# Joined narrow score products, earlier state products and moved operand making in a block of two SwiGLUs around retention and pooling

## The chip, the cores and the metric

The kernel runs on one core of a Trainium2 chip. The metric is the time of one execution in device microseconds. TensorE (PE, with PEld for its weight loads), VectorE (DVE), ScalarE (ACT) and SyncE (SP, which here only issues DMAs) each work through a queue of their own in order, and meet at semaphores.

## The reference

One layer of a streaming encoder over 1024 tokens of width 1024, all in float32:

```python
h = x + 0.5 * swiglu(rmsnorm(x), ffn1_w_in, ffn1_w_out)        # inner width 2816
u = rmsnorm(h)
q, k, v, g_ret, p, gates = split(u @ w_in)                     # 4 heads of 256
ret = retention(rotary(q), rotary(k) / 16, v)                  # chunks of 64, decay per head
ret = ret * rsqrt(mean(ret * ret) + eps) * silu(g_ret)         # norm per head
pool = multiscale_pool(p, pool_w, pool_scale)                  # windows 2, 4, 8, 16
merged = sum_b(sigmoid(gate_b) * (branch_b @ w_up_b))          # branches ret and pool
h = h + merged @ w_out
h = h + 0.5 * swiglu(rmsnorm(h), ffn2_w_in, ffn2_w_out)
out = rmsnorm(h)
```

## The kernel before

**Products.** Every float32 operand is split into a rounded part "hi" and the rest "lo" (`split`: a cast on ScalarE, L161, and a subtraction on VectorE, L162; `split_scaled`, L165 and L166, multiplies by a scale as well). A product is three matmuls that add into one PSUM bank (`mm3`, L181 to L183): hi·hi, hi·lo, lo·hi. Each matmul has its own weight load. Nearly all large products go through Strassen's scheme, so sums and differences of quarters are made on VectorE before they are split: R11, R12, R21, R22 are the quarters of a normed activation, and T1 to T4 are the differences made from them (class `Next`, L268 on).

**Stages**, by the times of the profile: first half of SwiGLU 1 to about 470 us; its second half, tiles named b..., to 630; the values v to 715; the projections q, k, gates and pool rows to 1154; retention, with the pooling products as filler, to 1345; the merge, groups `ru` and `wo`, to 1520; SwiGLU 2, tiles c..., to 1890, and its second half, tiles d..., to the end.

**The order of the work.** The kernel is written as generators of steps (prep, body). `Flow.run` calls each step's prep four steps ahead of its body (LOOK = 4), and after each body takes one or two items from a background queue (`flow.add`, `Next.work`): the making of the next stage's operands, stores, statistics. The instruction order that results is then scheduled; what is made under `soon()` gets a high priority. Tiles come from rings of buffers (`tl` 4, `t4` 9, `c2` 8, PSUM 6 and 2), so a load or an instruction that takes a buffer waits for the last reader of what lay in it.

**Retention** (class `Unit`, L1446 on). A unit is one head h and one half nh of the tokens of each span, named 00, 01, 10, ... 31: eight units. `scores` makes, for j = 0 and 1, the decayed scores `sm` of a block of 128 keys against 256 and 128 queries: products into a bank `s`, then `sc`, scores times decay from PSUM (L1529), then the split into `sm`. j = 1 is the narrow one: 12 matmuls 128 wide. `keys` transposes k (L1434) and splits it with its decay into `kd`, in halves of 256 columns, ACT then DVE. `update` makes the state product `st` from `kd` and v, adds it to the running state `sf` (L1569) and splits that into `state`. `products` runs `update` and then the outputs `ob`: state times q (`across`) and scores times v (`inner`). `retention` (L1649 on) puts them in order: scores, keys, a filler (`fill`, 24 matmuls of the pooling products `pu`), then the rest. `finish` transposes the outputs (`ot`) and multiplies them by the gate `rg`, which is loaded for it.

**Values** (`values`, L1251 on). The product L11 is followed by the products S2 and S1 in turn; their weights are sums made on VectorE (L1271 to L1273) in the tiles `vL` and `vS`, split into `vS2w`, `vS1w`. Meanwhile the background queue makes R21 and T4 of the activation `n2` (`n2R21`, `n2T4`), queued at the end of SwiGLU 1 (`end_of`, L1114).

**Merge.** `handed` queues, between the pairs of groups, the operands of the next stage: for `wo` from `ru` (`mg`), for SwiGLU 2 from `wo` (`n3`). Of the first pair of groups nothing is made before the second pair begins.

**Last half of SwiGLU 2** (`ffn_out`, with `last`). Products P1, P6, P2, P7, P5, then P3 (tiles `dp3m`, `dp3w`, into the banks `dp5a` that P5 leaves), then P4 as steps `near(k)` and `far(n)` into the banks `n4s`. When P5's banks are evacuated, VectorE makes `dd` from them.

Of the kernel before, what the change touches and what calls it, by code (L numbers as in the profile page):

```python
# [17 lines left out]
P = 128  # L18
# [72 lines left out]
def block_kernel(ctx: ExitStack, tc, x, x_tok, vecs, f1_in, f1_out, w_in, w_v, pool_w, w_ret, w_pool, w_o,  # L91
# [180 lines left out]
    class Next(Norm):  # L272


        def __init__(self, name, gain, keep=None):
            super().__init__(name)
            self.gain, self.keep = gain, keep
            self.M, self.Y, self.made, self.ready, self.tiles, self.t1s, self.rb = {}, {}, {}, set(), {}, {}, None

# [39 lines left out]

        def t2(self, i):  # L320
            R11, R12, R22 = self.tiles[i, 0], self.tiles[i, 1], self.tiles[i + 4, 1]
            t1 = self.t1s[i] = c2(f"{self.name}t1{i}")
            tt(t1, R12, R11, SUB)

            self.less(R11, R22, t1, i)
            self.put("T2", i, R11)

        def t1(self, i):
            self.put("T1", i, self.t1s.pop(i), self.g(i))

        def t3(self, i):
            R12, R22 = self.tiles[i, 1], self.tiles[i + 4, 1]
            self.less(R12, R22, R12, i)
            self.put("T3", i, R12)
# [487 lines left out]
    def ffn_out(nx, ops, ready, w, res, name, sink, end, last=None):  # L822
# [196 lines left out]
        for k in range(FH):  # L1019
            yield step("p3", p3, k, "a", False, after3)  # L1020
        if not last:
            for k in range(1, FH):
                yield step("p4", p4, k, "b", False, after4)
            return
# [33 lines left out]

        for k in range(FH):
            yield near(k)  # L1060
# [53 lines left out]
    def end_of(nx):  # L1114
        def end(part):
            if part == 4:
                nx.work(nx.r21, nx.t4_)
            else:
                nx.work(*{2: (nx.r11,), 5: (nx.r22, nx.p22), 3: (nx.t2, nx.t1, nx.t3)}[part])

        return end

    end1 = end_of(mix)


# [116 lines left out]
    def values():  # L1242
# [97 lines left out]
        for p in zip(product("S2", "T2", "a", False, after6), product("S1", "T1", "b", True, after5)):  # L1340
            yield from p
# [104 lines left out]
    class Unit:  # L1446


        def __init__(self, h, nh):
            self.h, self.nh, self.name = h, nh, f"{h}{nh}"  # L1450
# [61 lines left out]
        def scores(self):  # L1512

            self.sm = []
            for j in range(2):
                wid = SPAN - j * P
                b = bank(f"s{self.name}{j}")
                for s in range(2):
                    at = s * SPAN + j * P
# [6 lines left out]
                with soon():  # L1526
                    for s in range(2):
                        at = slice(s * wid, (s + 1) * wid)
                        stt(c[:, at], b[:, at], self.row(8, 2 * s + j), self.dec[:, :wid], MUL, MUL)  # L1529
# [51 lines left out]

        def products(self):
            self.ob = {}
            mid = self.update(0)
            if self.nh == 1:
                self.across(0, self.state)
            else:
                self.state = self.update(1)
            for s in range(2):
                self.inner(s)  # L1590
            self.across(1, mid)
# [49 lines left out]
    def retention():  # L1641
# [9 lines left out]
        for n, u in enumerate(units):  # L1651
            after = units[n + 1] if n + 1 < len(units) else None

            def scores(u=u, n=n):
                if u.nh == 1:
                    u.follow(units[n - 1])
                u.scores()

            def rest(u=u, after=after):
# [27 lines left out]
    def after(nx):  # L1687

        def t2(i):
            nx.r22(i)  # L1690
# [61 lines left out]
    def handed(nx, last):  # L1752
# [3 lines left out]
        def between(pair, n):  # L1756
            if pair == 0:
                return
# [203 lines left out]
```

## Time and profile before

| | |
|---|---|
| time, median of 3 runs (lowest, highest) | 2149.32 us (2148.17, 2150.93) |
| the profiled execution: its own time | 2149.24 us |
| its span in the profile | 2147.2 us |
| granted TensorE clock | 1.000 |
| busy: PE, PEld, DVE, ACT | 2134.6, 1812.8, 1871.7, 1100.8 us |
| chain that ended last | PE 93%, DVE 4% |

The profiled execution took 2.0 us more than its span, and it lies 0.08 us from the median. In the rows of the profile a matmul's duration is modelled and overlaps its neighbours: what a matmul costs in a row of matmuls is the distance from one start to the next.

### The profile page before, as it was taken

The page shows a single profiled execution, that of the slowest core. Times are in us where ns is not written, and L with a number is a line of the kernel's source. Part 1 is how long each engine was busy: PE and PEld are TensorE (multiplying, and loading weights), DVE is VectorE, ACT ScalarE, POOL GpSimd, SP SyncE. Part 2 cuts the span into 40 slices and gives each one's busy share as a digit, 9 for nine tenths or more (in the row PEclk, how much of TensorE's full clock was granted, in tenths as well). Part 3 has the DMA queues.
Part 4 walks back from the last instruction along what each step waited for, and adds up shares of the span by engine and source line. Part 5 has one row for each costly group of instructions (what it writes and reads, how often), then busy time and mean ns, then how long its engine had stood idle before and what let it go on. Part 6 is the DMA issues. An engine that isn't in the chain of part 4 may idle for free.

```text
span 2147.2 us, 30158 instructions
## 1 busy us (share of the span) xinstructions
PE 2134.6 (99%) x10830; PEld 1812.8 (84%) x10830; DVE 1871.7 (87%) x3344; ACT 1100.8 (51%) x2074; POOL 0.2 (0%) x4
## 2 busy tenths in 40 slices
PE   9999999999999999999999999999999999999998
PEld 7888888888887888888888888888888888888887
DVE  8798888997986799999988788899988988899796
ACT  8544444554653544545457653446644544455454
POOL 0000000000000000000000000000000000000000
PEclk9999999999999999999999999999999999999999
DMA  7232323585542333232337566624123232357542
GB/s 257 75 133 74 138 84 134 196 274 177 180 139 89 108 121 114 107 120 108 123 124 231 172 229 235 230 94 161 65 97 124 85 127 84 132 198 274 196 131 100
DMA packets 116102, 313.61 MB, mean 146 GB/s; under 512 B 12784, under 2 KB 17008, under 8 KB 115952
## 3 DMA queue, kind: packets, MB, share of 16 engines
q1 hardware_dynamic: 115376, 310.63, 41.9%
q8 instruction: 85, 1.39, 0.3%
q10 hardware_dynamic: 576, 1.05, 0.1%
q14 instruction: 65, 0.53, 0.1%
HBM read 220.93 MB, written 90.70 MB: 145 GB/s over the span
## 4 chain that ended last, share of the span: by engine, by line
PE 93%; DVE 4%; DMA 1%; ACT 1%; issue 0%; SPq 0%; DVEq 0%; ACTq 0%
PE c_b L181 2%; PE c_b L182 2%; PE c_b L183 2%; PE a_b L181 2%; PE a_b L182 2%; PE a_b L183 2%; PE c_e L181 2%; PE c_e L182 2%; PE c_e L183 2%; PE a_e L182 2%; PE a_e L181 2%; PE a_e L183 2%; PE a_a L181 1%; PE a_a L182 1%; PE a_a L183 1%; PE c_a L182 1%
## 5 line engine op out<-in xcount | busy, mean ns | idle before, releaser
L182 PE MATMUL c_b<-n3T,c_wS 128*128 128x512 f32 x176 | 68.6, 390 | 0.0
L183 PE MATMUL c_b<-n3T,c_wS 128*128 128x512 f32 x176 | 68.5, 389 | 0.0
L181 PE MATMUL c_b<-n3T,c_wS 128*128 128x512 f32 x176 | 68.2, 390 | 0.0
L181 PE MATMUL a_b<-n1T,a_wS 128*128 128x512 f32 x168 | 65.4, 389 | 0.0
L182 PE MATMUL a_b<-n1T,a_wS 128*128 128x512 f32 x168 | 65.4, 389 | 0.0
L183 PE MATMUL a_b<-n1T,a_wS 128*128 128x512 f32 x168 | 65.3, 389 | 0.0
L181 PE MATMUL a_a<-n1R,a_wL 128*128 128x512 f32 x120 | 46.7, 389 | 0.0
L182 PE MATMUL a_a<-n1R,a_wL 128*128 128x512 f32 x120 | 46.7, 389 | 0.0
L183 PE MATMUL a_a<-n1R,a_wL 128*128 128x512 f32 x120 | 46.7, 389 | 0.0
L182 PE MATMUL c_a<-n3R,c_wL 128*128 128x512 f32 x112 | 43.7, 390 | 0.0
L181 PE MATMUL c_a<-n3R,c_wL 128*128 128x512 f32 x112 | 43.6, 389 | 0.0
L183 PE MATMUL c_a<-n3R,c_wL 128*128 128x512 f32 x112 | 43.6, 389 | 0.0
L183 PEld LDWEIGHTS c_b<-n3T,c_wS 128*128 128x128 f32 x176 | 33.0, 188 | 6.9
L181 PEld LDWEIGHTS c_b<-n3T,c_wS 128*128 128x128 f32 x176 | 33.0, 188 | 6.7
L182 PEld LDWEIGHTS c_b<-n3T,c_wS 128*128 128x128 f32 x176 | 33.0, 188 | 6.6
L162 DVE TENSOR_TENSOR a_wS<-a_S,a_wS 128x512 fp32r<-128x512 f32 x45 | 30.6, 682 | 8.2 <-ACT a_wS L161 8.2
L183 PEld LDWEIGHTS a_b<-n1T,a_wS 128*128 128x128 f32 x168 | 31.5, 188 | 6.6
L181 PEld LDWEIGHTS a_b<-n1T,a_wS 128*128 128x128 f32 x168 | 31.5, 188 | 6.5
L182 PEld LDWEIGHTS a_b<-n1T,a_wS 128*128 128x128 f32 x168 | 31.5, 188 | 6.4
L162 DVE TENSOR_TENSOR c_wS<-c_S,c_wS 128x512 fp32r<-128x512 f32 x46 | 31.3, 682 | 3.7 <-ACT c_wS L161 3.6
L182 PE MATMUL c_e<-n3T,c_wL 128*128 128x512 f32 x88 | 34.5, 392 | 0.0
L181 PE MATMUL c_e<-n3T,c_wL 128*128 128x512 f32 x88 | 34.5, 392 | 0.0
(3378 smaller groups left out, 8145.1 us busy)
## 6 DMA issues: line engine op xcount, KB each, us to landing
c_ra<-in_f_in SPq DMA_DIRECT2D x22, 512.0 KB, 3.7
c_rb<-in_f_in SPq DMA_DIRECT2D x22, 512.0 KB, 3.7
a_ra<-in_f_in SPq DMA_DIRECT2D x21, 512.0 KB, 3.7
a_rb<-in_f_in SPq DMA_DIRECT2D x21, 512.0 KB, 3.7
t<-au SPq DMA_DIRECT2D x11, 512.0 KB, 2.9
b<-ag SPq DMA_DIRECT2D x11, 512.0 KB, 4.1
r<-au SPq DMA_DIRECT2D x11, 512.0 KB, 3.7
bra<-in_f_out SPq DMA_DIRECT2D x11, 512.0 KB, 5.5
```

What stands on the lines that cost most here:

```text
L162: tt(lo, src, hi.bitcast(F32), SUB)
L181: mm(dst, w[0], m[0], start=start, stop=False, skip_group_check=True)
L182: mm(dst, w[0], m[1], start=False, stop=False, skip_group_check=True)
L183: mm(dst, w[1], m[0], start=False, stop=stop, skip_group_check=True)
```

## The change

Five edits:

1. **Joined scores.** For j = 1, `scores` no longer calls `mm3`: hi of the weights is multiplied by hi and lo of the queries side by side, one matmul 256 wide, and lo by hi, one 128 wide, adds to its first half. The two halves of the bank are then added: a copy on ACT of the second half to `sc`, an addition on DVE; decay is applied to the sum in SBUF.
2. **State products early.** For the units n ≥ 3 (11, 20, 21, 30, 31) the order is keys, scores, updates, filler, where it was scores, keys, filler, updates.
3. **Values.** R21 and T4 of n2 (8 items) are queued at the third step of S2 and S1, not at the end of SwiGLU 1.
4. **Merge.** At the end of the first pair, `handed` queues for i = 0, 1 the scaling of R22 and two differences (`sum1`, `sum3`), which T1, T2 and T3 then use.
5. **Last SwiGLU.** `near(0)`, P4's first step, comes before P3, the others after; its operands T4 and L22 are loaded k = 0 alone and then in pairs.

```diff
 def t2(self, i):
-            R11, R12, R22 = self.tiles[i, 0], self.tiles[i, 1], self.tiles[i + 4, 1]
-            t1 = self.t1s[i] = c2(f"{self.name}t1{i}")
-            tt(t1, R12, R11, SUB)
-
-            self.less(R11, R22, t1, i)
+            self.sum1(i)
+            R11, R22 = self.tiles[i, 0], self.tiles[i + 4, 1]
+            self.less(R11, R22, self.t1s[i], i)
             self.put("T2", i, R11)
...
-            at = (k + (key in ("T4", "L22") and not last)) % 2
+            at = (k + (key in ("T4", "L22"))) % 2
...
+        yield near(0)
         for k in range(FH):
+            yield step("p3", p3, k, "a", False, after3)
+        for k in range(1, FH):
             yield near(k)
...
-        for p in zip(product("S2", "T2", "a", False, after6), product("S1", "T1", "b", True, after5)):
+        for k, p in enumerate(zip(product("S2", "T2", "a", False, after6), product("S1", "T1", "b", True, after5))):
+            if k == 2:
+                nx.work(nx.r21, nx.t4_)
             yield from p
...
-                        mm3(b[:, s * wid : (s + 1) * wid], parts(self.K[i], slice(at, at + P)),
-                            parts(self.Q[i], slice(at, at + wid)), s == 0 and i == 0, i == 1)
+                        w, m = parts(self.K[i], slice(at, at + P)), self.Q[i][:, :, at : at + wid]
+                        first, final = s == 0 and i == 0, i == 1
+                        if j == 0:
+                            mm3(to, w, (m[:, 0], m[:, 1]), first, final)
+                        else:
+                            mm(to, w[0], m, start=first, stop=False, skip_group_check=True)
+                            mm(to[:, :P], w[1], m[:, 0], start=False, stop=final, skip_group_check=True)
...
+                    if j:
+                        both, src = b.rearrange("p (s z c) -> p s z c", s=2, z=2), c
+                        sums = c[:, :n].rearrange("p (s c) -> p s c", s=2)
+                        copy(sums, both[:, :, 1])
+                        tt(sums, both[:, :, 0], sums, ADD)
...
-            yield none, scores
-            yield none, u.keys
+            if n < 3:
+                yield none, u.scores
+                yield none, u.keys
+            else:
+                yield none, u.keys
+                yield none, u.scores
+                yield none, u.updates
             yield from fill()
...
         def between(pair, n):
             if pair == 0:
+                if n == BY_OPERAND[-1]:
+                    flow.add(*(lambda m=m, i=i: m(i) for i in range(2) for m in (nx.r22, nx.sum1, nx.sum3)))
                 return
```

**Unit 11 on TensorE.** Before, after the transposes `ot` of head 0, come the scores, of which the last three narrow matmuls stand here, the four transposes of k, and then the filler `pu1`:

```order
L181 MATMUL s111_11742<-q111_11630,k111_11636 128x128
L182 MATMUL s111_11742<-q111_11630,k111_11636 128x128
L183 MATMUL s111_11742<-q111_11630,k111_11636 128x128
L1434 MATMUL kd11b0_11761<-cst_68,k11_11421 128x128 x4
L700 MATMUL pu1d0_11771<-po00_10991,pu1w0_11652 128x512
L701 MATMUL pu1d0_11771<-po00_10991,pu1w0_11652 128x512
```

Of the change, the transposes stand ahead of the scores (twelve matmuls `s110`, of which the last stands here); the eight joined ones, of which four stand here, and the first of the twelve state products `st110` follow, then the filler.

```order
L1441 MATMUL kd11b0_11717<-cst_68,k11_11417 128x128 x4
...
L183 MATMUL s110_11727<-q111_11624,k111_11630 128x256
L1533 MATMUL s111_11746<-q110_11621,k110_11627 128x256
L1534 MATMUL s111_11746<-q110_11621,k110_11627 128x128
L1533 MATMUL s111_11746<-q111_11624,k111_11630 128x256
L1534 MATMUL s111_11746<-q111_11624,k111_11630 128x128
...
L181 MATMUL st110_11763<-v110_11547,kd110_11718 128x256
```

The state products stand right behind the scores, ahead of 24 matmuls of filler that used to lie between; twelve narrow matmuls are eight.

**Unit 11 on VectorE.** Before, the lower parts of `kd110` (two halves) stand behind the scores of the unit, and the gate products `rg00` come later:

```order
L1529 SCALAR_TENSOR_TENSOR sc110_11736<-s110_11723,by1_11301,dec1_11143 128x256 x2
L162 TENSOR_TENSOR sm110_11737<-sc110_11736,sm110_11737 128x512
L1529 SCALAR_TENSOR_TENSOR sc111_11755<-s111_11742,by1_11301,dec1_11143 128x128 x2
L166 SCALAR_TENSOR_TENSOR kd110_11762<-kd11b0_11761,by1_11301,kd110_11762 128x256
L162 TENSOR_TENSOR sm111_11756<-sc111_11755,sm111_11756 128x256
L162 TENSOR_TENSOR v200_11802<-v20_11682,v200_11802 128x512
L166 SCALAR_TENSOR_TENSOR kd110_11762<-kd11b0_11761,by1_11301,kd110_11762 128x256
L162 TENSOR_TENSOR v201_11805<-v20_11682,v201_11805 128x512
L162 TENSOR_TENSOR q200_11883<-q20_11684,q200_11883 128x512
L1622 TENSOR_TENSOR rg00_11693<-ot000_11695,rg00_11693 128x512
L1622 TENSOR_TENSOR rg00_11693<-ot010_11701,rg00_11693 128x512
```

Of the change:

```order
L1419 TENSOR_TENSOR pg0_11499<-pu0d0_11521,pg0_11499 128x512
L1419 TENSOR_TENSOR pg0_11499<-pu0d1_11522,pg0_11499 128x512
L1645 TENSOR_TENSOR rg00_11676<-ot000_11678,rg00_11676 128x512
L1645 TENSOR_TENSOR rg00_11676<-ot010_11684,rg00_11676 128x512
L1645 TENSOR_TENSOR rg01_11691<-ot001_11693,rg01_11691 128x512
L166 SCALAR_TENSOR_TENSOR kd110_11718<-kd11b0_11717,by1_11297,kd110_11718 128x256
L1645 TENSOR_TENSOR rg01_11691<-ot011_11699,rg01_11691 128x512
L1547 SCALAR_TENSOR_TENSOR sc110_11740<-s110_11727,by1_11297,dec1_11141 128x256 x2
L166 SCALAR_TENSOR_TENSOR kd110_11718<-kd11b0_11717,by1_11297,kd110_11718 128x256
L162 TENSOR_TENSOR v200_11807<-v20_11706,v200_11807 128x512
L1544 TENSOR_TENSOR sc111_11755<-s111_11746,sc111_11755 128x256
```

The gate products `rg00` and `rg01` now stand ahead of `kd110`, and the addition `sc111` (L1544) is new. On SyncE the loads of `rg00` and `rg01` now stand ahead of that of v20, right behind pg2; before they stood behind k20, pm0 and pg3. The load of k20 now stands behind the stores `ret0` and `ret1` of those gate products.

**The values on VectorE.** Before, around the weights `vS2w2` of the third S2 step, the making of `n2T4` and the scaled sums `bacc` lie between:

```order
L162 TENSOR_TENSOR vS1w1_6110<-vS21_6083,vS1w1_6110 128x512
L162 TENSOR_TENSOR n2T40_6134<-bacc4_4363,n2T40_6134 128x512
L347 SCALAR_TENSOR_TENSOR bacc5_4364<-bacc5_4364,vec_66,bacc1_4360 128x512
L1271 TENSOR_TENSOR vS22_6141<-vS22_6141 128x512
L347 SCALAR_TENSOR_TENSOR bacc6_4365<-bacc6_4365,vec_66,bacc2_4361 128x512
L162 TENSOR_TENSOR n2T41_6138<-bacc5_4364,n2T41_6138 128x512
L1272 TENSOR_TENSOR vS22_6141<-vL112_5976,vS22_6141 128x512
L162 TENSOR_TENSOR n2T42_6163<-bacc6_4365,n2T42_6163 128x512
L1273 TENSOR_TENSOR vL112_5976<-vS22_6141,vL112_5976 128x512
L347 SCALAR_TENSOR_TENSOR bacc7_4366<-bacc7_4366,vec_66,bacc3_4362 128x512
L1271 TENSOR_TENSOR vS23_6189<-vS23_6189 128x512
L162 TENSOR_TENSOR vS2w2_6147<-vL112_5976,vS2w2_6147 128x512
```

Of the change:

```order
L1277 TENSOR_TENSOR vS22_6121<-vL112_5976,vS22_6121 128x512
L166 SCALAR_TENSOR_TENSOR n2R210_6142<-bacc4_4363,vec_66,n2R210_6142 128x512
L162 TENSOR_TENSOR vS2w1_6083<-vL110_5935,vS2w1_6083 128x512
L162 TENSOR_TENSOR vS1w1_6098<-vS21_6077,vS1w1_6098 128x512
L1278 TENSOR_TENSOR vL112_5976<-vS22_6121,vL112_5976 128x512
L166 SCALAR_TENSOR_TENSOR n2R211_6145<-bacc5_4364,vec_66,n2R211_6145 128x512
L166 SCALAR_TENSOR_TENSOR n2R212_6167<-bacc6_4365,vec_66,n2R212_6167 128x512
L162 TENSOR_TENSOR vS2w2_6127<-vL112_5976,vS2w2_6127 128x512
L162 TENSOR_TENSOR vS1w2_6148<-vS22_6121,vS1w2_6148 128x512
L166 SCALAR_TENSOR_TENSOR n2R213_6170<-bacc7_4366,vec_66,n2R213_6170 128x512
L1276 TENSOR_TENSOR vS23_6173<-vS23_6173 128x512
```

`vS2w2` comes nine rows earlier, ahead of `n2R213` and of all of `n2T4`.

**From P5 to P3 on TensorE.** Before, P3 follows the last matmuls of P5:

```order
L181 MATMUL dp5a3_19507<-dp5m10_19689,dp5w10_19686 128x512
L182 MATMUL dp5a3_19507<-dp5m10_19689,dp5w10_19686 128x512
L183 MATMUL dp5a3_19507<-dp5m10_19689,dp5w10_19686 128x512
L181 MATMUL dp5a0_19504<-dp3m0_19718,dp3w0_19715 128x512
L182 MATMUL dp5a0_19504<-dp3m0_19718,dp3w0_19715 128x512
L183 MATMUL dp5a0_19504<-dp3m0_19718,dp3w0_19715 128x512
```

Of the change, six matmuls of P4 into `n4s0` and `n4s1` lie between:

```order
L183 MATMUL dp5a3_19491<-dp5m10_19673,dp5w10_19670 128x512
L181 MATMUL n4s0_19584<-dp4w0_19701,dp4m0_19704 128x512
L182 MATMUL n4s0_19584<-dp4w0_19701,dp4m0_19704 128x512
L183 MATMUL n4s0_19584<-dp4w0_19701,dp4m0_19704 128x512
L181 MATMUL n4s1_19622<-dp4w0_19701,dp4m0_19704 128x512
L182 MATMUL n4s1_19622<-dp4w0_19701,dp4m0_19704 128x512
L183 MATMUL n4s1_19622<-dp4w0_19701,dp4m0_19704 128x512
L181 MATMUL dp5a0_19488<-dp3m0_19729,dp3w0_19726 128x512
L182 MATMUL dp5a0_19488<-dp3m0_19729,dp3w0_19726 128x512
```

On VectorE the splits `dp3m9` and `dp3m10`, which stood ahead of the four `dd` of P5, now stand behind them.

More of the change, by code (lines that the diff above doesn't have):

```diff
@@ L1018, in ffn_out @@
             yield step("p4", p4, 0, "b", False, after4)
-        for k in range(FH):
-            yield step("p3", p3, k, "a", False, after3)
-        if not last:
+            for k in range(FH):
+                yield step("p3", p3, k, "a", False, after3)
             for k in range(1, FH):
@@ L1112, in block_kernel, with end1 @@
     mix = Next("n2", V_MIX, h1)
[L1114 to L1123, printed above, removed]
+    def end1(part):
+        mix.work(*{2: (mix.r11,), 5: (mix.r22, mix.p22), 3: (mix.t2, mix.t1, mix.t3)}.get(part, ()))
     tab, stored = {}, set()
@@ L1665, in rest @@
                     u.normalise()
-            yield none, scores
-            yield none, u.keys
+                else:
+                    after.follow(u)
+            if n < 3:
+                yield none, u.scores
+                yield none, u.keys
+            else:
+                yield none, u.keys
+                yield none, u.scores
+                yield none, u.updates
             yield from fill()
@@ L1689, in t2 @@
         def t2(i):
-            nx.r22(i)
+            if i not in nx.t1s:
+                nx.r22(i)
             nx.t2(i)
```

40 lines of the change are left out of this document (25 added, 15 removed).

## The prediction

> **What bounds the kernel now.** I read the page first, then the list of what TensorE waited for, then single stretches of the timeline around each wait. The page says who sets the time:
>
> ```profile
> PE 2134.6 (99%) x10830; PEld 1812.8 (84%) x10830; DVE 1871.7 (87%) x3344; ACT 1100.8 (51%) x2074; POOL 0.2 (0%) x4
> PE 93%; DVE 4%; DMA 1%; ACT 1%; issue 0%; SPq 0%; DVEq 0%; ACTq 0%
> ```
>
> TensorE is busy 99% of the span and makes 93% of the chain. So only two things can shorten the run: fewer or cheaper matmuls, or one of the few waits of TensorE closed. The list of waits names the second kind:
>
> ```profile
> PE vL L181 <- ACT vS2w L161: 1.5, 1, 1.5
> ...
> PE ob L182 <- DVE state L162: 1.1, 2, 0.8
> PE ob L181 <- ACT state L161: 0.6, 2, 0.5
> ...
> PE wo0e L183 <- DVE wo0wS L162: 0.4, 1, 0.4
> PE wo1b L183 <- DVE wo1wS L162: 0.4, 1, 0.4
> PE dp5a L181 <- DVE dd L953: 0.2, 1, 0.2
> ```
>
> Edits 2 to 5 each aim at a line of this list; together the lines hold 4.2 us. I work each out by start-to-start distances, since idle counts only from a matmul's modelled end. All sums are made against the profiled execution, 2149.24 us, which is its span of 2147.2 plus 2.0 around it and practically the median.
>
> **1. Joined scores.** Narrow score matmuls, by shape, and the starts in unit 11 (two wide ones, the first two narrow, the transpose that follows the twelfth):
>
> ```profile
> L181 PE MATMUL s<-q,k x64: 222/277/364, 1154.1 to 1306.0; 128*128 128x256 f32 x32, 128*128 128x128 f32 x32
> ```
>
> ```profile
> 1226.98 0.28 PE L183 MATMUL s<-q,k 128*128 128x256 f32 x1
> 1227.10 0.22 PE L181 MATMUL s<-q,k 128*128 128x128 f32 x1
> 1227.16 0.28 PE L182 MATMUL s<-q,k 128*128 128x128 f32 x1
> ...
> 1228.39 0.62 PE L1434 MATMUL kd11b<-cst,k 128*128 128x128 f32 x4
> ```
>
> Each of three lines has 32 narrow matmuls, 96 in all, 12 in each of 8 units. Twelve take 1228.39 − 1227.10 = 1.29 us, 0.11 each; a 256-wide one takes 0.12 (1226.98 to 1227.10). So a narrow matmul costs almost what a wide one does. Of the change, four wide and four narrow take 4 × 0.12 + 4 × 0.11 = 0.92 us: 0.37 less per unit, **3.0 us** for eight. Bounds: 0, if the joined ones cost by their columns, and 3.5, if the four that go cost 0.11 each.
>
> The first narrow one took 0.06 us until the next start, so the columns alone don't set the 0.11. [...]
>
> What is added, an ACT copy and a DVE addition of 256 columns per unit (like kinds below take 0.47), lies beside TensorE's work, except where VectorE has no pause (part 3).
>
> **2. Values.** TensorE, VectorE, ScalarE around the wait:
>
> ```profile
> 653.06 0.39 PE L183 MATMUL vS<-vS1w,n2T 128*128 128x512 f32 x1
> 654.93 1.20 PE L181 MATMUL vL<-vS2w,n2T 128*128 128x512 f32 x4 [1.48 <-ACT vS2w L161]
> ```
>
> ```profile
> 653.55 0.68 DVE L1273 TENSOR_TENSOR vL<-vS,vL 128x512 f32<-128x512 f32 x1
> ```
>
> ```profile
> 654.26 0.62 ACT L161 CAST vS2w<-vL 128x512 fp32r<-128x512 f32 x1 [1.78 <-DVE vL L1273]
> ```
>
> The distance is 1.87 us where 0.23 is usual: 1.64 lost. The cast waited for VectorE, which was working through the making of n2's operands. In the change `vS2w2` stands nine rows earlier; at about 0.6 us a row that is 5 us for a wait of 1.64. Next late would be `vS4w0`, some 11 us later; its row has not moved back. I take **1.7** with the 0.1 that trails a wait; bounds 0 and 1.8. The moved R21 and T4 are needed only by the last two products, some 30 us on.
>
> **3. Retention.** Unit 01 first: TensorE, then VectorE, rows left out between.
>
> ```profile
> 1194.40 0.28 PE L183 MATMUL ob<-v,sm 128*128 128x256 f32 x1
> 1194.84 0.39 PE L181 MATMUL ob<-state,q 128*128 128x256 f32 x1 [0.16 <-ACT state L161]
> 1195.99 0.39 PE L182 MATMUL ob<-state,q 128*128 128x256 f32 x1 [0.77 <-DVE state L162]
> ```
>
> ```profile
> 1190.94 0.68 DVE L162 TENSOR_TENSOR pw<-pw,pw 128x512 fp32r<-128x512 f32 x1
> 1191.53 0.68 DVE L162 TENSOR_TENSOR pu0w<-pu0raw,pu0w 128x512 fp32r<-128x512 f32 x1
> ...
> 1194.05 1.28 DVE L162 TENSOR_TENSOR v<-v,v 128x512 fp32r<-128x512 f32 x2
> 1195.26 0.68 DVE L162 TENSOR_TENSOR state<-sf,state 128x512 fp32r<-128x512 f32 x1
> ```
>
> Lost: (0.44 − 0.12) + (1.15 − 0.12) = 1.35. The four splits in these VectorE rows (2.4 us) now stand behind `state`; the new addition (0.4) stands ahead. `state` comes 2.0 us earlier, the wait goes, and `sm`, which has gone behind `sf`, may cost 0.15: **1.2**, bounds 0 and 1.45.
>
> Units 11 and 21 wait for `state` too. Unit 11's wait on TensorE:
>
> ```profile
> 1239.39 0.38 PE L181 MATMUL ob<-state,q 128*128 128x256 f32 x1
> 1240.12 0.39 PE L182 MATMUL ob<-state,q 128*128 128x256 f32 x1 [0.34 <-DVE state L162]
> ```
>
> That is 0.73 − 0.12 = 0.6; unit 21's is the longest of its line in the list, 0.5. There the state product now has a filler behind it, 24 matmuls or 5.4 us, so `state` is in time. What is late next is `kd`, which used to have that filler as cover. TensorE in unit 11, then ScalarE, then VectorE, and the same ends in unit 21:
>
> ```profile
> 1228.77 0.48 PE L700 MATMUL pu1d<-po,pu1w 128*128 128x512 f32 x1
> ```
>
> ```profile
> 1229.05 0.47 ACT L165 ACTIVATE kd<-kd11b,by 128x256 fp32r<-128x256 f32 x1 [0.22 <-PE kd11b L1434]
> ```
>
> ```profile
> 1231.67 0.48 DVE L166 SCALAR_TENSOR_TENSOR kd<-kd11b,by,kd 128x256 fp32r<-128x256 f32 x1
> ```
>
> ```profile
> 1267.41 0.48 PE L700 MATMUL pu2d<-po,pu2w 128*128 128x512 f32 x1
> ```
>
> ```profile
> 1271.43 0.47 DVE L166 SCALAR_TENSOR_TENSOR kd<-kd21b,by,kd 128x256 fp32r<-128x256 f32 x1
> ```
>
> The transposes end where the filler starts, at 1228.77 and 1267.41; the second half of `kd` is whole at 1232.15 and 1271.90: 3.4 and 4.5 us. Of the change it is needed after the scores (1.44 + 0.92 = 2.36) and five state products (0.6): 2.96. At the pace of before 0.4 and 1.5 would be lost; in unit 21 the new order takes rotary work of about 1.2 us out from between. I take 0.4 and 0.3. Net: 11 gains 0.6 − 0.4 = **0.2**, 21 gains 0.5 − 0.3 = **0.2**. The other three of these units had no such wait to lose; their `kd` chains come out 0 to 0.5 late.
>
> VectorE then works without a real pause from unit 21 to unit 31:
>
> ```profile
> 1263.21 2.48 DVE L1622 TENSOR_TENSOR rg<-ot,rg 128x512 f32<-128x512 f32 x4 [5.17 <-PE ot L1621]
> ...
> 1301.42 1.28 DVE L162 TENSOR_TENSOR k<-k,k 128x512 fp32r<-128x512 f32 x2
> ```
>
> ```profile
> 1303.50 0.36 PE L181 MATMUL s<-q,k 128*128 128x256 f32 x1
> ```
>
> Unit 31's keys are split at 1302.7, its scores start at 1303.5: 0.8 to spare. TensorE gets about 1.2 us faster over these units (2 × 0.37 of scores and the wait of 21), VectorE gets two additions more and one filler split less. So some 0.5 of what is gained comes back as a wait in unit 31: **−0.5**, bounds 0 and −1.5.
>
> **4. Merge: 0.** The additions made early move inside one stretch in which VectorE has no pause, and as many of its instructions (86) stand between the last evacuation of `ru1` and the late `wo1wS` as before. The waits of `wo0e` and `wo1b` stay; if they went, 2.0 with what trails them (0.8 in the list).
>
> **5. Last SwiGLU.** TensorE and VectorE where P5 meets P3:
>
> ```profile
> 2078.30 0.39 PE L183 MATMUL dp5a<-dp5m,dp5w 128*128 128x512 f32 x1
> 2078.88 0.47 PE L181 MATMUL dp5a<-dp3m,dp3w 128*128 128x512 f32 x1 [0.20 <-DVE dd L953]
> ```
>
> ```profile
> 2077.44 0.69 DVE L162 TENSOR_TENSOR dp3m<-dR,dp3m 128x512 fp32r<-128x512 f32 x1 [1.28 <-ACT dp3m L161]
> ```
>
> P3 waits for banks, 0.58 − 0.23 = 0.35 and a further 0.3 a few matmuls on: `dd` stood behind a `dp3m` that came late. Now six matmuls of P4 (6 × 0.23 = 1.4) lie between, and `dp3m9` and `dp3m10` stand behind `dd`. **0.6**, bounds 0 and 0.7; P4's first operands are split on VectorE right behind the last of P5 (two rows, 1.2 us), and P5's last twelve matmuls (12 × 0.23 = 2.7 us) cover that.
>
> **Sum**: 3.0 + 1.7 + 1.2 + 0.2 + 0.2 − 0.5 + 0 + 0.6 = 6.4, and 0.5 for the distances of 0.1 to 0.3 that go with closed waits and were left out: 6.9. 2149.24 − 6.9 = **2142.3 us**.
>
> **The rivals.**
>
> *VectorE takes the retention gains back.* From unit 21 on TensorE can't run ahead of VectorE; if unit 01's wait only moves as well, half the scores (1.5), the values (1.7), P3 (0.6) and 0.4 are left: 4.2, 2145.0 us. For it: VectorE without pause for 39 us. Against: the 0.8 to spare and the 5.17 us of idle ahead. Chance 0.20.
>
> *The joined matmuls cost by their columns.* Then the 3.0 go: 2145.3. Against: 0.11 beside 0.12 in these rows. Chance 0.06. [...]
>
> *The merge waits go too*: 2.0 more, 2140.3. Against: equally many VectorE rows ahead. Chance 0.10.
>
> *The edit of the values doesn't do what it says*: the wait turns up again at `vS4w0`; 2144.0. Chance 0.04.
>
> *Slower: head 0's gate products hold up unit 11.* VectorE, then SyncE's queue:
>
> ```profile
> 1234.40 1.29 DVE L1622 TENSOR_TENSOR rg<-ot,rg 128x512 f32<-128x512 f32 x2 [1.05 <-DMA rg<-g]
> ```
>
> ```profile
> 1206.69 0.32 SPq L140 DMA_DIRECT2D v<-v  x1
> ```
>
> `rg00` waited for its load until 1234.40. Three `rg` products now stand ahead of `kd110` on VectorE, and behind that the state products, the filler and all else on TensorE. If the load lands as late as before, `kd110` is whole at about 1237.9 (1234.40 + 1.8 + two scores 0.8 + 2 × 0.47) and was needed at 1229.0: 8.9 us lost, 2151.2 us. It decides from a landing after 1225.2 on, and eats the whole gain from about 1232. Against: the load now stands ahead of v20's, which was issued at 1206.69; from there 18 us remain. Chance 0.05.
>
> **How the numbers follow.** Forecast 0.55, rivals 0.20, 0.06, 0.10, 0.04, 0.05. The range 2139.8 to 2146.0 takes in the merge rival below, VectorE's and the columns' above with the bound of −1.5 in part 3; the slower case and the tails are left out. A measurement of this kernel tells about 0.2% (4.3 us) from no change: faster means below 2145.0. The forecast, the merge and the values case lie there, with half of VectorE's: 0.55 + 0.10 + 0.04 + 0.10 = 0.79, and 0.01 of the columns. Slower is 0.03 of the last rival, where the load is later still; the rest, 0.17, is the same.
>
> **What would show it.** In the profile of the change: narrow and joined scores 0.92 us a unit from first start to the next kind; no line `vL <- vS2w`; the lines `ob <- state` gone and lines `st <- kd` of a few tenths in their place, `s <- k` or `st` in unit 31 about 0.5; `wo` lines as before; no wait between `n4s` and `dp3m`. I am wrong where `rg` waits for a DMA ahead of `kd110`, where joined scores take 1.2 us or more, or where a new wait of over 1 us stands in retention.

## The result and the profile after

The change takes 2142.57 us (median of six runs, 2140.69 to 2143.74) against 2149.69 of before (six runs, 2148.17 to 2152.45): ratio 0.9965, 95% interval 0.9954 to 0.9977. The forecast was 2142.3. The profiled execution took 2143.71 us, 2141.8 of it the span; by its two profiles 5.4 us of span are gained, less than by the medians, because this execution is one of the two longest of its six.

The page of the change first, the two lines on busy time and on the chain:

```profile
PE 2129.9 (99%) x10798; PEld 1809.6 (84%) x10798; DVE 1874.0 (87%) x3352; ACT 1103.3 (52%) x2082; POOL 0.2 (0%) x4
PE 91%; DVE 6%; DMA 1%; ACT 1%; issue 1%; SPq 0%; ACTq 0%; DVEq 0%
```

TensorE has lost 32 matmuls and 4.7 us of busy time. But in the chain VectorE has gone up from 4% to 6%. The list of what TensorE waited for (total, times, longest; the lines left out are the kernel's first matmuls) says where:

```profile
PE ru1b L183 <- DVE ru1wS L162: 1.9, 1, 1.9
...
PE wo0e L183 <- DVE wo0wS L162: 0.4, 1, 0.4
...
PE c_x L182 <- DVE n3R22y L162: 0.2, 1, 0.2
PE st L182 <- DVE v L162: 0.2, 1, 0.2
PE px L181 <- DVE po L166: 0.2, 1, 0.2
```

The lines of `vL`, of `ob` and of `dp5a` are gone, and at the top stands one that was not there before: `ru1b`, the start of the merge. The values' stretch, 630 to 715 us, as a row of the windows view (length, then PE busy):

```profile
630.00:715.00 85.00, 85.00 (x383) 70.29 (x382) 59.83 (x108) 37.42 (x66) 0.00 (x0) 1.00 0.31 102
```

It was busy 83.5 us of 85 before and has no idle now. The narrow scores of unit 11 on TensorE, where L1533 is a joined matmul and L1534 a narrow one:

```profile
1223.29 0.28 PE L1533 MATMUL s<-q,k 128*128 128x256 f32 x1
1223.41 0.22 PE L1534 MATMUL s<-q,k 128*128 128x128 f32 x1
1223.47 0.34 PE L1533 MATMUL s<-q,k 128*128 128x256 f32 x1
1223.65 0.23 PE L1534 MATMUL s<-q,k 128*128 128x128 f32 x1
...
1224.17 0.34 PE L181 MATMUL st<-v,kd 128*128 128x256 f32 x1
...
1224.69 0.28 PE L182 MATMUL st<-v,kd 128*128 128x256 f32 x1
1224.96 0.39 PE L183 MATMUL st<-v,kd 128*128 128x256 f32 x1
```

The eight take 1224.17 − 1223.29 = 0.88 us where the twelve took 1.29: 0.41 less, as in units 10, 20 and 21, or 3.3 us if all eight units are alike (in three the scores stand mixed with other matmuls). The last two rows are the second half of `kd`: 0.27 from start to start, so the matmul came 0.15 late.

Now the balance along TensorE's rows, before minus after, at the same matmul of both profiles: 1.9 us gained behind the values (0.1 of it from the kernel's first matmuls), 2.2 at the start of retention, 7.1 at its end, 5.1 behind the new wait in `ru1b`, 5.65 at the end of `wo`, 4.8 behind the first half of SwiGLU 2, 5.4 at the end. So the change earned 7 us by the end of retention and handed 2 of them to one wait at the start of the merge.

That wait, and what stands behind it. SyncE's issue of the load of `ru1rb`, one of the eight loads of the `ru` weights; what the DMA view says of it (the last number is us from issue to landing); VectorE; TensorE:

```profile
1356.88 0.33 SPq L140 DMA_DIRECT2D ru1rb<-in_w_ret  x1
```

```profile
ru1rb<-in_w_ret SPq DMA_DIRECT2D x1, 512.0 KB, 5.6
```

```profile
1360.35 0.69 DVE L162 TENSOR_TENSOR ruT<-ret,ruT 128x512 fp32r<-128x512 f32 x1
1362.55 0.69 DVE L455 TENSOR_TENSOR ru1S<-ru1rb 128x512 f32<-128x512 f32 x1 [1.50 <-DMA ru1rb<-in_w_ret]
...
1366.88 0.69 DVE L162 TENSOR_TENSOR ru1wS<-ru1S,ru1wS 128x512 fp32r<-128x512 f32 x1
```

```profile
1365.30 0.39 PE L182 MATMUL ru1b<-ruT,ru1wS 128*128 128x512 f32 x1
1367.62 0.50 PE L183 MATMUL ru1b<-ruT,ru1wS 128*128 128x512 f32 x1 [1.94 <-DVE ru1wS L162]
```

The list blames VectorE, but VectorE itself had stood idle for 1.50 us for the load. 2.32 − 0.23 = 2.09 us are lost on TensorE. The buffer of `ru1rb` held the eighth pooling gate `pg7` first, so the load is issued only behind that gate's last store. In the kernel before, the same load and the same instruction of VectorE:

```profile
1363.36 0.38 SPq L140 DMA_DIRECT2D ru1rb<-in_w_ret  x1
```

```profile
1367.87 0.69 DVE L444 TENSOR_TENSOR ru1S<-ru1rb 128x512 f32<-128x512 f32 x1
```

There VectorE came to `ru1S` without idle, and TensorE met its operand with nothing to spare: it started 0.32 us behind the matmul ahead of it, where 0.23 is usual. In the change TensorE could have started this matmul 7.4 us earlier and VectorE `ru1S` 6.8 us earlier; the issue is 6.5 earlier and the landing only 5.3.

### The profile page after: what moved, and what is told of

The parts are those of the page before. It is cut to its first block, busy times and chain, and to the rows that moved or that the text cites. A ratio compares the mean times of both kernels' runs of the same rounds, so it can differ in the third digit from the quotient of the medians.

```text
span 2141.8 us, 30121 instructions
## 1 busy us (share of the span) xinstructions
PE 2129.9 (99%) x10798; PEld 1809.6 (84%) x10798; DVE 1874.0 (87%) x3352; ACT 1103.3 (52%) x2082; POOL 0.2 (0%) x4
## 3 DMA queue, kind: packets, MB, share of 16 engines
q10 hardware_dynamic: 576, 1.05, 0.1%
## 4 chain that ended last, share of the span: by engine, by line
PE 91%; DVE 6%; DMA 1%; ACT 1%; issue 1%; SPq 0%; ACTq 0%; DVEq 0%
PE a_b L181 2%; PE a_b L182 2%; PE a_b L183 2%; PE c_b L181 2%; PE c_b L182 2%; PE c_b L183 2%; PE c_e L182 2%; PE c_e L181 2%; PE c_e L183 2%; PE a_e L181 2%; PE a_e L182 2%; PE a_e L183 2%; PE a_a L181 1%; PE a_a L183 1%; PE a_a L182 1%; PE c_a L181 1%
## 5 line engine op out<-in xcount | busy, mean ns | idle before, releaser
L182 PE MATMUL c_e<-n3T,c_wL 128*128 128x512 f32 x88 | 34.5, 394 | 0.0
L161 ACT CAST c_wS<-c_S 128x512 fp32r<-128x512 f32 x46 | 28.0, 626 | 12.7 <-DVE c_S L455 7.1
L181 PE MATMUL c_e<-n3T,c_wS 128*128 128x512 f32 x88 | 34.4, 391 | 0.0
```

Of the source, the lines that this page charges most:

```text
L161: copy(hi, src)
L181: mm(dst, w[0], m[0], start=start, stop=False, skip_group_check=True)
L182: mm(dst, w[0], m[1], start=False, stop=False, skip_group_check=True)
```

## The experiments

The times of before are the medians of the runs on the same chip. Edits 1 to 5 are those of the change.

**e1: joined scores alone.** The state of before with this edit only.

```diff
-                        mm3(b[:, s * wid : (s + 1) * wid], ...)
+                            mm(to, w[0], m, start=first, stop=False, skip_group_check=True)
+                            mm(to[:, :P], w[1], m[:, 0], start=False, stop=final, skip_group_check=True)
```

> The kernel before with the joined scores alone. Theory (a narrow score matmul is paid by its weight load): the narrow group of a unit takes 0.88 us for 1.29, 3.3 us in eight units; the lists of the scheduler also put four splits behind the state of unit 01, so its wait of 1.35 us goes: about 2149.5 - 4.6 = 2145 us. The waits of units 11 and 21 for the state (0.6 and 0.6), of vL (1.6) and of wo (1.9) stay. Rival (VectorE takes the gain back through the eight additions): the groups are as short, but new waits of TensorE for VectorE stand in units 21 to 31 and the time is 2147 or more.

Measured: 2146.90 us against 2149.07, ratio 0.9993, interval 0.9983 to 1.0002. In unit 11 the eight matmuls start 0.12 and 0.06 apart, then 0.17 and 0.06, as in the change. So the matmuls became as much cheaper as in the change, and the total hardly shows it. The waits do, in the list of this run:

```profile
PE ru1a L181 <- ACT ru1b L481: 1.8, 1, 1.8
...
PE ru1b L183 <- DVE ru1wS L162: 1.4, 1, 1.4
```

Both are new; by the distances they cost 1.94 and 1.55 us. ScalarE had waited 4.96 us for the load of `ru1ra` (5.9 us from issue to landing), and VectorE behind it for ScalarE:

```profile
1357.66 0.69 DVE L162 TENSOR_TENSOR ru1wL<-ru1ra,ru1wL 128x512 fp32r<-128x512 f32 x1 [1.93 <-ACT ru1wL L161]
```

From there VectorE had no pause up to `ru1S`, and all of its rows came late: `ret`, for which ScalarE waited 3.08 us with the copy of the first line queued behind, and `ru1S`, which is behind the second line. The profiled execution is the longest of the ten (2150.60), so these two waits stand for it and not for the median. The wait of unit 01 for its state is gone in this run as well, though nothing in this edit moves the state.

**e2: edits 2 to 5, without joined scores.** The reverse of the diff of e1.

> The change without the joined scores (the four other edits). Theory: narrow groups take 1.29 us again, the vL wait is gone (1.7), the state waits of 11 and 21 are gone with 0.3 each in their place, P3 gains 0.4: about 2149.5 - 3 = 2146.5 us, and 3.3 to 4.5 us above the whole change. Rival (the other edits need the scores' room on VectorE): kd is late by 0.5 or more in each of the five later units, 2148.5 or more.

Measured: 2145.86 us, ratio 0.9983, interval 0.9974 to 0.9992. Against the change's ratio the joined scores are worth 0.0018 of 2149 us, about 3.9; the intervals laid against each other leave anything from 0 to 8. In the profile (2149.01, the longest of the ten) unit 01 waits for its state again, 0.69 and 1.04 us, while units 11 and 21 don't; unit 30 has two new waits, 0.73 us for the transposes of k and 0.46 in its scores.

**e3: the change, with the load of `ru1rb` freed from `pg7`.** The eighth gate gets a buffer of another ring.

```diff
-                gate[mt] = raw(f"pg{mt}")
+                gate[mt] = (wide if mt == KT - 1 else raw)(f"pg{mt}")
```

> The whole change, with the tile of the last pooling gate in another ring of buffers, so that the load of ru1rb no longer waits for the store of that tile. Theory (the new wait of ru1b, 2.1 us, is VectorE's 1.5 us of idle for the load of ru1rb): the load is issued several us earlier, VectorE's idle ahead of ru1S goes, and the wait of ru1b falls to 0.6 or less: 2142.6 - 1.6 = 2141 us. Rival (VectorE is simply late with ru1wS because TensorE comes earlier): the load comes earlier and the wait of ru1b stays at 1.5 us or more, 2142.6 us.

Measured: 2141.09 us (2140.11 to 2141.47), ratio 0.9962, interval 0.9948 to 0.9976. The load is issued at 1345.4 now, 11.5 us earlier; the loads of `ru0ra`, `ru0rb` and `ru1ra`, whose buffers shift with it, are issued 5 to 9 us earlier, and the scheduler puts VectorE's `ru1S` at 1350.5. So this run tests the buffer, with all that hangs on it. The list of TensorE's waits, again without the kernel's first matmuls:

```profile
...
PE wo0e L183 <- DVE wo0wS L162: 0.4, 1, 0.4
...
PE st L182 <- DVE v L162: 0.2, 1, 0.2
PE s L1533 <- DVE rg L1645: 0.2, 1, 0.2
```

No line `ru1b`. This is the lowest median of the study; its interval overlaps the change's, but its five runs lie within 1.4 us where the change's six are spread over 3.1. The total alone would not tell the theory from the rival; the missing line does.

**e4: both score matmuls 256 wide.** The second matmul also takes hi and lo side by side, which adds lo by lo: the same count of matmuls as the change, twice the columns in half of them.

```diff
-                            mm(to[:, :P], w[1], m[:, 0], start=False, stop=final, skip_group_check=True)
+                            mm(to, w[1], m, start=False, stop=final, skip_group_check=True)
```

> The whole change, but the second matmul of each joined pair is 256 wide as well: lo of the weights times hi and lo of the queries, so the small lo x lo product is added, which the change leaves out. Theory (two weight loads set a pair's time, whatever its width): the eight matmuls of a unit take 0.88 to 0.96 us, and the time stays within 0.7 us of the change, 2142.6 to 2143.3. Rival (the columns set it: 0.235 us for 384 columns): 0.31 us a pair, 1.25 us a unit, 3 us more, 2145.6 us.

Measured: 2149.05 us, ratio 1.0002, interval 0.9992 to 1.0011. Both readings missed the total. The group itself, unit 11 on TensorE:

```profile
1225.60 0.28 PE L1533 MATMUL s<-q,k 128*128 128x256 f32 x1
1225.72 0.28 PE L1534 MATMUL s<-q,k 128*128 128x256 f32 x1
...
1226.56 0.28 PE L181 MATMUL st<-v,kd 128*128 128x256 f32 x1
```

0.96 us for eight, 0.08 more than in the change; by their columns the four wider ones would take 4 × 0.06 = 0.24 more. Eight units make 0.6 us. The other 6 us are waits elsewhere: the instruction order came out differently (a weight tile `pw` of the pooling, 2.4 us late in unit 00), and the loads of the merge were issued at 1353.5 and 1363.6 instead of 1345.5 and 1356.9, which costs 2.4 us in `ru1a`, 1.75 in `ru1b`, and 1.6 through the clock (last section). With the change's own 2.1 in `ru1b` taken off and the 0.6 added, these make 6.6. Between the medians lie 6.5 us, between the two profiles only 5.4 of span, so smaller differences elsewhere go the other way. The total says nothing about columns here; the group does.

**e5: before, with the early load only.** The edit of e3 in the kernel before.

> The kernel before, with only the eighth pooling gate in another buffer, so that the load of ru1rb no longer waits for that gate's store. Theory (the early load is worth only what the ru1b wait costs, and before has no such wait): 2148.3 to 2149.9, the waits of the merge as before. Rival (the early load is a gain of its own, whatever stands ahead of it): about 1.5 us less, 2147.0 to 2148.0.

Measured: 2149.45 us against 2149.26, ratio 1.0001, interval 0.9991 to 1.0010. In the merge there was little for the early load to win: before loses 0.2 us at `ru1b`, this run none. Its profiled execution (2151.01) has a wait of 2.13 us in unit 21, 0.63 in before, and a slower clock behind it (last section), so the total is no clean measure here either. What it does show is no gain of 1.5 us.

**e6: joined scores alone, with the early load.** The diffs of e1 and e3 in one.

> Joined scores alone, with the early load. Theory (the joined scores save 3.3 us on TensorE and the loads of ru1ra and ru1rb that come late, 1.94 and 1.55 us in the run with joined scores alone, take it back): both waits gone, 2143.0 to 2145.0. Rival (the joined scores save little, and the run with them alone showed what they are worth): 2146.0 to 2147.2.

Measured: 2145.15 us, ratio 0.9978, interval 0.9969 to 0.9988; just above the theory's range, and outside the rival's. The list of this run has neither `ru1a` nor `ru1b`:

```profile
PE vL L181 <- ACT vS2w L161: 1.5, 1, 1.5
...
PE wo1b L183 <- DVE wo1wS L162: 0.4, 1, 0.4
PE wo0e L183 <- DVE wo0wS L162: 0.4, 1, 0.4
```

Against e5 this is 4.3 us, near the sum of the scores' 3.3 and unit 01's wait of 1.35. In e1 the merge had taken some of it, 1.75 us between the medians.

**e7: the change without edit 4 (merge).**

```diff
-                if n == BY_OPERAND[-1]:
-                    flow.add(*(lambda m=m, i=i: m(i) for i in range(2) for m in (nx.r22, nx.sum1, nx.sum3)))
```

> The change without the edit to the first merge's differences (late load as in the change). Theory (that edit is worth nothing, and the new ru1b wait comes from TensorE being some 7 us ahead of a load that follows the last pooling store): ru1b waits 1.5 to 2.3 us here too, 2141.8 to 2143.4. Rival (the moved differences delay the merge's VectorE work): no ru1b wait, 2140.0 to 2141.3.

Measured: 2143.01 us (2141.62 to 2146.45), ratio 0.9971, interval 0.9961 to 0.9982. In the total the edit is worth nothing that can be measured. In the list one line comes back that the change does not have, `wo1b` with 0.4, as before; the waits of `wo` lose 2.0 us by the distances, as before, and 1.4 in the change. And the wait in `ru1b` is 0.60 us here, between theory and rival. VectorE's instructions in this place are in the same order as in the change, and the load is issued at the same time, 1356.86; it lands after 4.1 us instead of 5.6. That raised the question that e12 answers.

**e8: the change without edit 2 (early states), with the early load.** To be read against e3.

```diff
-            if n < 3:
-                yield none, u.scores
-                yield none, u.keys
-            else:
-                yield none, u.keys
-                yield none, u.scores
-                yield none, u.updates
+            yield none, u.scores
+            yield none, u.keys
```

> The change without the early states, with the early load; compared with the change with the early load, 2141.1. Theory (the early states are worth the state waits of units 01, 11 and 21 less a give-back in unit 31, 1.1 us net): waits for a state of over 0.9 us in sum in units 01 to 21, 2141.9 to 2143.0. Rival (the joined scores alone already take the wait of unit 01 away, as in the run with them alone, and only 0.4 us of state waits is left for the early states): 2140.8 to 2141.8.

Measured: 2142.23 us against 2141.09 of e3 (ratio to before 0.9967, interval 0.9954 to 0.9980). The total is the theory's (the intervals of e8 and e3 overlap, so the rows must decide), the place is not. The expectation gave the edit unit 01's state, which it does not touch. No wait for a state is left in units 01 to 21. All of the difference stands in unit 31; TensorE's waits there:

```profile
1297.05 0.39 PE L181 MATMUL s<-q,k 128*128 128x256 f32 x1 [0.33 <-ACT k L161]
1297.94 0.38 PE L183 MATMUL s<-q,k 128*128 128x256 f32 x1 [0.26 <-DVE k L162]
1311.74 0.39 PE L182 MATMUL ob<-state,q 128*128 128x256 f32 x1 [0.29 <-DVE state L162]
```

By the distances 0.49, 0.43 and 0.46, where e3 has 0.33: 1.05 us, and 1.4 with the distances that trail these waits.

**e9: edit 3 (values) alone.**

```diff
-                nx.work(nx.r21, nx.t4_)
+            if k == 2:
+                nx.work(nx.r21, nx.t4_)
```

> Of the change only the values' part (R21 and T4 of n2 put off until the second pair of products). Theory: the wait of vL for vS2w goes and nothing takes its place at vS4w0, 1.64 us by the distances, so 2147.0 to 2148.0. Rival (the wait turns up again at vS4w0 or in the merge): 2148.4 to 2149.6.

Measured: 2147.59 us against 2149.64, ratio 0.9991, interval 0.9982 to 1.0001: the theory's time, though not clear of no change. The line of `vL` is gone, and again a new one stands in the merge, 1.31 us by the distance:

```profile
PE ru1b L183 <- DVE ru1wS L162: 1.2, 1, 1.2
```

This edit lies 700 us ahead of the merge and moves no instruction of it. In this execution unit 01 had no wait either (why, under e10); TensorE would have come to `ru1b` 3.6 us earlier than in before, and 1.31 of that is taken there. VectorE came to `ru1S` 2.3 us earlier, and had no idle there: the load landed at 1365.53, `ru1S` started at 1365.55, 0.61 us behind the row ahead of it, where 0.60 is usual. So the load and VectorE's own queue meet in this place, and no run parts them.

**e10: edit 2 (early states) alone.** The reverse of the diff of e8, in the kernel before.

> Of the change only the early states. Prediction's reading (this edit moves the state of unit 01 ahead of the four splits): no wait for the state in unit 01, 11 or 21, 2146.8 to 2147.8. Theory now (the joined scores, not this edit, brought the state of unit 01 forward, through the order that VectorE then got): 1.0 to 1.8 us of wait for the state stays in unit 01, those of units 11 and 21 go, 2147.9 to 2149.0.

Measured: 2148.79 us, ratio 0.9997, interval 0.9988 to 1.0007. The waits of units 11 and 21 are gone, 0.54 us have turned up in `ru1b` (VectorE without idle there, as in e9), 0.73 and 0.46 in unit 30, and unit 01 still waits, by the distances 0.80 and 1.04 us. Why, shows ScalarE, and VectorE behind it; first e10:

```profile
1181.61 0.62 ACT L161 CAST pw<-pw 128x512 fp32r<-128x512 f32 x1 [1.69 <-DMA pw<-in_pool_w]
```

```profile
1182.86 1.41 DVE L166 SCALAR_TENSOR_TENSOR po<-px,vec,po 128x512 fp32r<-128x512 f32 x2 [1.92 <-ACT po L165]
...
1193.64 0.68 DVE L1569 SCALAR_TENSOR_TENSOR sf<-sf,st 128x512 f32<-128x512 f32 x1
```

The cast of `pw` waits 1.69 us for its load; `po` behind it on ScalarE is late, VectorE idles 1.92 us for that, and `sf` starts 3.1 us behind the last matmul of the state product (1190.51). Now e1, and e9's answer to the same question:

```profile
1184.69 0.62 ACT L161 CAST pw<-pw 128x512 fp32r<-128x512 f32 x1
```

```profile
1190.86 0.69 DVE L1580 SCALAR_TENSOR_TENSOR sf<-sf,st 128x512 f32<-128x512 f32 x1
```

```profile
pw<-in_pool_w SPq DMA_DIRECT2D x1, 256.0 KB, 3.0
```

With joined scores alone the scheduler puts that cast 3 us later, so ScalarE does not wait, and `sf` runs 2.8 us earlier, right behind the state product (whose last matmul starts at 1190.54). In e9 the order is that of before, but this one load took 3.0 us where it took 4.3 in the profile of before and 4.9 here, and nothing waits. Over the profiles with this order the wait follows the load: 3.0 us go with none, 4.3 (before, e5) with 1.35 and 1.2, 4.6 (e2, e11) with 1.7, 4.9 with 1.84. So unit 01's wait too is a load that came late, and edit 1's order takes it out of the way.

**e11: edit 5 (P4's first step) alone.**

```diff
+        yield near(0)
         for k in range(FH):
+            yield step("p3", p3, k, "a", False, after3)
+        for k in range(1, FH):
             yield near(k)
```

> Of the change only P4's first step ahead of P3 in the last SwiGLU. Theory: the wait of dp5a goes and 0.3 to 0.6 us with it, 2148.4 to 2149.0; a total that small can hardly be told from none, so the distances between the starts of dp5a in the trace decide (all under 0.3 us where P5 meets P3). Rival (the wait only moves to n4s or dp3m): a distance of over 0.45 us there.

Measured: 2148.99 us, ratio 0.9997, interval 0.9988 to 1.0007: not to be told from none. On TensorE, where P5, P4's first step and P3 meet:

```profile
2078.93 0.39 PE L183 MATMUL dp5a<-dp5m,dp5w 128*128 128x512 f32 x1
2079.16 0.39 PE L181 MATMUL n4s<-dp4w,dp4m 128*128 128x512 f32 x1
...
2080.29 0.39 PE L183 MATMUL n4s<-dp4w,dp4m 128*128 128x512 f32 x1
2080.52 0.39 PE L181 MATMUL dp5a<-dp3m,dp3w 128*128 128x512 f32 x1
```

All distances are 0.23: the 0.35 of before and the 0.3 behind it are gone. In the change 0.26 of the latter are left.

**e12: the change once more**, to settle e7.

No line differs.

> The change itself once more, for a second profile of the same instructions. Theory (the third product of ru1b starts 5.07 us after VectorE first touches ru1rb, TensorE has to wait 0.6 us for VectorE's own queue, and the 1.5 us more in the first profile are the load, 5.67 us from issue to landing where 4.1 would have been in time): ru1S starts 1361.0 to 1362.6, the wait by the distance is 0.5 to 2.1 us and equals ru1S's start plus 5.07 less 1365.5, and a load of 4.1 us or less goes with 0.6 us. Rival (the wait of 2.1 us is fixed by this kernel's order, whatever the load takes): 2.0 to 2.2 us with a load under 5 us. Total 2141 to 2144.

Measured: 2141.63 us (2140.28 to 2142.75), ratio 0.9965, interval 0.9953 to 0.9978. The same rows as in the first profile, from a second execution of the same instructions: DMA (issued at 1356.79), VectorE, TensorE.

```profile
ru1rb<-in_w_ret SPq DMA_DIRECT2D x1, 512.0 KB, 4.1
```

```profile
1360.88 0.69 DVE L455 TENSOR_TENSOR ru1S<-ru1rb 128x512 f32<-128x512 f32 x1
```

```profile
1365.23 0.39 PE L182 MATMUL ru1b<-ruT,ru1wS 128*128 128x512 f32 x1
1365.96 0.50 PE L183 MATMUL ru1b<-ruT,ru1wS 128*128 128x512 f32 x1 [0.34 <-DVE ru1wS L162]
```

1365.96 − 1360.88 = 5.08, as in the first profile (1367.62 − 1362.55 = 5.07), in e7 and in e9. The wait is 0.73 − 0.23 = 0.50 with a load of 4.1 us, 2.09 with one of 5.6. So 0.5 to 0.6 of it is VectorE's own queue (in e12 the load landed 0.02 us before VectorE took it up, without idle), and the rest is the length of the one load in that execution. The spans differ by 2.0 us, most of it this.

## Why the prediction was right, point by point

The total is right, 2142.57 for 2142.3, and two errors of opposite sign lie in it: more was won up to the end of retention than was worked out, and some of it was lost in the merge. So the hit to 0.3 us is luck in part; how much was lost hangs on the length of one load. The 7.1 us between the medians lie between the two profiles, 5.4 us of span in the first and 7.4 in e12.

**1. Joined scores, 3.0.** Right, a little small: 0.88 for 0.92 us per unit, 3.3 us. The rival by which they cost their columns is out, by the group in e4 and by the totals of e6 against e5. Behind the first, a pair takes 0.23 to 0.24 us, whether its second matmul is 128 or 256 wide. The weight loads start 0.11 to 0.12 us apart beside these matmuls, in the change as in before; that they set the time, as the expectations of e1 and e4 have it, is the author's reading, and no run shows it apart from the count of matmuls.

**2. Values, 1.7.** Right: 1.64 us by the wait, 1.8 by the balance, and nothing late at `vS4w0`; e9.

**3. Retention, 1.2 + 0.2 + 0.2 − 0.5.** The waits of units 01, 11 and 21 went as worked out, `kd` came 0.26 and 0.34 late by the rows where 0.4 and 0.3 were taken, and unit 31 lost 0.31 where 0.5 was taken. Unit 21's wait was 0.63 by the distance, where the list's 0.5 was taken. That part brought about 1.6 us (7.1 at the end of retention, less 2.2 at its start and 3.3), where 1.1 and some of the 0.5 for trailing distances stood. The prediction read unit 01 off VectorE's order in the whole change and left open which edit makes it: joined scores do. And the four splits ahead of `state`, on which it put the wait, were not what made it: they stand there in e9 too, without a wait. The late load of `pw` made it, through ScalarE and `po` (e1, e9, e10). It booked VectorE's −0.5 in unit 31 as the price of the edits together; e8 shows that the early states lower that price, from 1.4 to 0.3 us. The rival in which VectorE takes the retention gains back did not come: TensorE could run ahead of VectorE there.

**4. Merge, 0.** This step failed, in both directions. For the edit itself 0 is what the total of e7 shows, but the merge as a place lost 0.5 to 2.1 us in `ru1b`. The prediction counted VectorE's rows ahead of the late `wo` weights and took it that VectorE has no pause there. It did not ask when VectorE's own operands land if all that stands ahead is done 7 us earlier. The place had nothing to spare in the profile of before, and the load, chained to a store, came 6.5 us earlier at its issue and 5.3 at its landing where TensorE could have come 7.4.

The count of rows misled in the other direction as well. The rival that the waits of `wo` go too was right in part: they went from 2.0 to 1.4 us by the distances. The line `wo1b` is missing in all six runs with edit 4 (the change, e2, e3, e4, e8, e12) and stands in all eight without it. From the last evacuation of `ru1` to the late `wo1wS` VectorE has as many rows as before, as predicted, but it takes 51.4 us with the edit (the change, e12) and 52.1 without (before, e7): three distances of 0.71, 0.76 and 0.96 us between rows have become the usual 0.60.

**5. Last SwiGLU, 0.6.** Right in place: 0.45 us at P3 and 0.14 at the last sum; e11 alone 0.7.

**The rest.** Between the merge and the last half of SwiGLU 2 the first profile loses 0.8 us, most of it in distances of 0.1 to 0.4 us more than usual at `c_x`, which e12 shows too and e3's list does not. That is about what edit 4 wins at `wo`. What sets them is not shown: e2, e3, e4 and e8 have edit 4 as well, and lose only 0.14 at the longest of these places, where the change loses 0.38.

**Slower: `rg`.** No such wait came; the only one is 0.2 to 0.3 us in unit 31.

By the rows of the first profile, then: 2.2 + 3.3 + 1.6 = 7.1 in place of 5.8 up to the end of retention, 2.0 lost in `ru1b` (0.5 in e12), 0.6 won at `wo`, 0.8 lost in SwiGLU 2, 0.6 won at its end, or 5.4 in all by the unrounded rows.

## What to carry to other kernels

When TensorE is to arrive somewhere earlier, look past the edit for the next place that has nothing to spare, loads above all: here a load that waits for a store to free its buffer was issued 6.5 us earlier where TensorE could have come 7.4, and part of what was gained ahead of it was lost there. The change lost 1.6 us so in one execution and e1 3.5 in another; in e9 and e10 the load and VectorE's queue met in the same place, and 1.3 and 0.5 us were lost. Read a wait through: if the engine that is blamed stood idle itself, the cause is what it waited for. Count time, not rows: as many instructions took 0.6 us less here. Where a scheduler makes the order, a total does not tell what a single edit is worth; the rows of the group do.

## What the runs showed of the hardware that was not expected

**The clock after a wait of 2 us.** In e4 TensorE waited at the start of `ru1a`, and then for a while its matmuls started 0.42 to 0.43 us apart instead of 0.23:

```profile
1355.42 0.39 PE L183 MATMUL ru0a<-ruR,ru0wL 128*128 128x512 f32 x1
1357.60 0.50 PE L181 MATMUL ru1a<-ruR,ru1wL 128*128 128x512 f32 x1 [1.80 <-ACT ru1wL L161]
...
1359.36 0.61 PE L183 MATMUL ru1a<-ruR,ru1wL 128*128 128x512 f32 x1
1359.78 0.63 PE L181 MATMUL ru1a<-ruR,ru1wL 128*128 128x512 f32 x1
...
1362.76 0.41 PE L182 MATMUL ru0a<-ruR,ru0wL 128*128 128x512 f32 x1
```

The windows view gives the granted clock behind the brackets of POOL:

```profile
1359.40:1362.80 3.40, 3.40 (x10) 2.62 (x9) 3.40 (x7) 0.84 (x3) 0.00 (x0) 0.50 0.32 131
```

Half the clock for 3.4 us, with 0.99 in the 1.9 us ahead and 1.00 in the 3.2 behind: 1.6 us lost on top of the wait, which is 1.95 us by the distance. The profile of e5 has the same behind a wait of 2.13 us in unit 21 (0.51 over 3.4 us); the change's wait of 2.09 us and e1's of 1.94 were followed by the full clock (1.00 from 1345 to 1380 in the change, from 1360 to 1376 in e1). So was, by its matmuls 0.23 to 0.24 us apart, the wait of 2.4 us for `pw` in e4 itself. The length of the wait alone does not part the five cases, and what does is not shown. In two of them a wait of about 2 us cost nearly twice its own length.

**A load's length.** The 512 KB of `ru1rb`, issued at the same time by the same instructions, took 5.6 us in one execution and 4.1 in another; the 256 KB of unit 01's `pw` took 3.0 to 4.9 in the executions of this study. Each decided a wait of 1 to 2 us.
